# New SBUF start addresses for the operand tiles of the matrix products in a two-layer hybrid decoder

## The chip, the cores and the metric

The kernel runs on one core of a Trainium2 chip. The metric is device time in microseconds (us) of one execution: the median of three runs of the kernel before is 1026.87 us (1026.75 to 1027.55).

## The reference

A trunk of two layers on 256 tokens with 1024 channels, all in float32. Layer 0 mixes tokens with two recurrences (RG-LRU and HGRN2), layer 1 with a Mamba-2 state-space mixer. Each layer then has cross-attention into 256 memory tokens and a squared-ReLU MLP. Nearly all arithmetic is products of a 256-row activation with weight matrices:

```python
for l in range(DEPTH):                                   # 2 layers
    h = rmsnorm(x, norm_mix_g[l])
    if l % 2 == 0:
        proj = h @ e_w_in[e]                             # 1024 x 6144
        ...                                              # rg_lru, hgrn2_mix
        mix = jnp.concatenate([ya, yb], axis=-1) @ e_w_out[e]     # 2048 x 1024
    else:
        z, xbc, dt_raw = jnp.split(h @ o_w_in[o], O_SPLITS, axis=-1)
        ...                                              # mamba2_mix
        mix = ym @ o_w_out[o]                            # 2048 x 1024
    x = x + mix
    x = x + mem_cross_attn(rmsnorm(x, ...), rmsnorm(mem, ...), xq_w[l], xk_w[l], xv_w[l], xo_w[l])
    hf = rmsnorm(x, norm_ffn_g[l])
    x = x + jnp.square(jax.nn.relu(hf @ ffn_w1[l])) @ ffn_w2[l]   # 1024 x 4096, 4096 x 1024
return rmsnorm(x, final_norm_g)
```

## The kernel before

**Operands in two parts.** Every float32 operand of a large product is split in two float32r numbers, high and low, so that a product is three matmuls: high x high, high x low, low x high. A weight half-chunk (128 partitions x 1024 numbers, 512 KiB) is loaded by SyncE's queue into a tile `raw` (`Stream.loading`, line 150). ScalarE copies it into `wh` (line 164) and VectorE subtracts to make `wl` (line 165). There are four `raw` buffers and five each of `wh` and `wl`; loads and splits run a fixed number of halves ahead of the products. Activations are split in the same way into `nh`, `nl` (normalized inputs of a block, four buffers each) and `yh`, `yl` (outputs of mixers, attention and MLP, eight buffers each). Each such buffer holds two tiles of 128 x 256, 2 KiB per partition.

**The products.** `gemm` (lines 451, 453, 454) keeps 128 columns of a weight part in the array and streams 256 tokens of an activation part past them: for each k-tile of 128 channels and each 128 columns, one matmul with `wh` and the high activation part, one with `wh` and the low part, one with `wl` and the high part. Each of them loads its weights anew. `gemm_nat` (lines 470 to 472) turns this around: 128 tokens of an activation part are stationary and 512 columns of a weight part stream. A weight half-chunk has 24 matmuls of the first kind or 12 of the second. The order of the instructions is made by the framework's scheduler from the program's order, with short chains of steps put between the products; inside a product it is fixed (`seq`).

**Where tiles lie.** Pools take SBUF in the order in which they are opened: `cst` (constants, the residual stream `xres`), `wp` (`raw`, `wh`, `wl`), `ap` (all other working tiles), then `l0` or `l1` (one layer's own). Within a pool each buffer follows the one before. So the constants decide where the weight tiles begin. In the built program, in bytes along a partition:

| tiles | first buffer at | each buffer | start modulo 512 | modulo 64 |
|---|---|---|---|---|
| `raw`, `wh`, `wl` (pool `wp`) | 30,272 | 4,096 | 64 | 0 |
| `yh`, `yl` (pool `ap`) | 108,128 | 2,048 | 96 | 32 |
| `nh`, `nl` (pool `ap`) | 177,024 | 2,048 | 384 | 0 |

A matmul reads 512 bytes (128 stationary numbers) and 1,024 or 2,048 bytes (256 or 512 streamed numbers) per partition, and these pieces start at the tile's start plus a multiple of 512.

Of the kernel before, what the change touches and what calls it, by code (L numbers as in the profile page):

```python
# [16 lines left out]
P = 128  # L17
D = 1024
T = 256
# [5 lines left out]

# halves of weight chunks: buffers as loaded and as split, how far ahead they are split, and loaded before that
RAW_BUFS, PART_BUFS, SPLIT_AHEAD, LOAD_AHEAD = 4, 5, 3, 4
# chunks of layer 1's memory keys and values before the groups of the state-space mixer, and with each of them
KV_FIRST, *KV_EACH = 2, 2, 2, 2, 0, 0, 0, 0, 0
# how far short chains are taken ahead of the program's order  # L30
AHEAD = 200

# ---------------------------------------------------------------- the order of the weight chunks
# A chunk is 128 x (kt * cols) with kt * cols = 2048 (or less): kt k-tiles of a block of columns.

# [72 lines left out]

# ---------------------------------------------------------------- columns of the table of small parameters
_FIRST = [("memkv", 16), ("mix", 16)]  # L110
# [15 lines left out]
class Stream:  # L126
    """The halves of the weight chunks in their order: load, and split in two float32r parts."""

# [14 lines left out]
    def loading(self):  # L143
        """the next half, a piece at a time"""
        h = self.loaded
        self.loaded += 1
        hk, n = self._shape(h)
        self.raw[h] = raw = self.pool.tile([P, 1024], F32, tag="raw", bufs=RAW_BUFS, name=f"raw{h // 2}_{h % 2}")
        for a, b in self._pieces(h, hk * n):
            self.nc.sync.dma_start(raw[:, a:b], self.wst[h // 2, h % 2, :, a:b])  # L150
            yield
# [27 lines left out]
    def ahead(self, h):  # L179
        """what goes on while half h is multiplied"""  # L180
        with self.tc.high_priority(offset=0):
            self.split(h + 1 + SPLIT_AHEAD)
            self.load(h + 1 + SPLIT_AHEAD + LOAD_AHEAD)
# [7 lines left out]
class Pipe:  # L191
    """Chains of small steps that are issued a step at a time between the large products."""

# [19 lines left out]
def trunk(ctx: ExitStack, tc: tile.TileContext, wst, small, levels, gatew, xT, memT, fing, out):  # L213
# [3 lines left out]
    cst = ctx.enter_context(tc.tile_pool(name="cst", bufs=1))  # L217
    wp = ctx.enter_context(tc.tile_pool(name="wp", bufs=1))
    ap = ctx.enter_context(tc.tile_pool(name="ap", bufs=1))
    ps = ctx.enter_context(tc.tile_pool(name="ps", bufs=1, space=PSUM))  # L220
# [10 lines left out]
    def sc(i, name, shape=(P, 2, 256)):  # L231
        """scratch, two tiles of 2 KiB for each number"""
        return gt(name, f"s{i}", 2, shape)

    def nhl():
        return gt("nh", "nh", 4, dt=F32R), gt("nl", "nl", 4, dt=F32R)

    def yhl():
        return gt("yh", "yh", 8, dt=F32R), gt("yl", "yl", 8, dt=F32R)

# [25 lines left out]

    onesr = cst.tile([P, 128], F32R, name="onesr")
    def xpair(p):
        return xres[:, 2 * p:2 * p + 2, :]

    # ---------------------------------------------------------------- small helpers
    def seq():
        return tc.manual_schedule(engines={PE.engine})

    def order(after, before, why):
        """two instructions of one engine, in this order"""
        tc.add_manual_dep(after.ins, before.ins.name, NOSYNC, reason=why)
# [19 lines left out]
    def diag(r):  # L297
        """diagonal matrices of the two columns of r, in two parts"""
        dh, dl = (gt(t, t, 2, (P, 2, 128), F32R) for t in ("dgh", "dgl"))
        with tc.high_priority(offset=AHEAD):  # L300
            for j in range(2):
                V.tensor_scalar(dh[:, j, :], ident, r[:, j:j + 1], None, ALU.mult)
            for j in range(2):
                V.scalar_tensor_tensor(dl[:, j, :], ident, r[:, j:j + 1], dh[:, j, :].bitcast(F32),
                                       ALU.mult, ALU.subtract)
        return dh, dl
# [10 lines left out]
    def token_sums(sq, o, fold):  # L317
        """o[:, half] = the sum over channels of sq [channels, 2, tokens]"""
        n = 1 if fold else 2
# [27 lines left out]
    def gained(hl, src, gain, i0):  # L347
        """src * gain (a column for each of the two tiles) in two parts"""
        h, lo = hl
# [6 lines left out]
    class Norm:  # L356
        """x * gain in two float32r parts, and 1 / rms of every token."""

# [18 lines left out]
        def add(s, xp, p, parts=True):  # L377
            """a chain of steps for one pair of tiles"""
            parts = parts and s.gain is not None
# [33 lines left out]
        def apply(s, xp, p):  # L413
            """the norm applied before the projection"""
            h = sc(3, "hx")
# [9 lines left out]

    # ---------------------------------------------------------------- products with the weights
    def chunk(label, piece, ticks=1, rows=1):
# [14 lines left out]
    def gemm(label, os, H, L, k0=0, first=True, last=True, ticks=1):  # L442
        """os[pair][:, j, :] += W[:, 128 columns of each]^T x over the k-tiles of a chunk"""
        kt = PLAN[st.pos][3]
# [19 lines left out]
    def gemm_nat(label, os, H, L, k0=0, first=True, last=True, ticks=1):  # L464
        """os[half] += x[tokens of the half]^T W over the k-tiles of a chunk, tokens on partitions"""
        kt = PLAN[st.pos][3]
# [8 lines left out]

    # ---------------------------------------------------------------- memory keys and values
    kT, vN = [[], []], [[], []]

    class Memory:
# [13 lines left out]
        def step(s, ticks=1):  # L493
            """the next chunk of the keys, then of the values"""
            i, l, n = s.done, s.l, s.n
# [76 lines left out]

    # ---------------------------------------------------------------- parameters of layer 0's mixers
    def pt():
# [33 lines left out]
    def conv(o, wn, bn, tiles, stride, cv):  # L608
        """width-4 causal depthwise convolution of two tiles"""
        r = sc(cv, "cv")  # L610
# [7 lines left out]

    # ---------------------------------------------------------------- RG-LRU
    def rglru(p, xc, ga):  # L620
# [33 lines left out]

    # ---------------------------------------------------------------- HGRN2
    sts = []
# [8 lines left out]
    def hgrn(p, F, K, q, Q, vg):  # L665
        """scores by halves of blocks of 2, 4, ... 256 tokens; every decay is a product of forget gates"""
        Qf, Kf, Tm = flat(Q), flat(K), flat(F)
# [114 lines left out]

    # ---------------------------------------------------------------- parts that both layers have
    def residual(o, p, nrm):
# [6 lines left out]
    def out_deep(label, H, L, nrm, ticks=1):  # L791
        """x += W^T y, 16 k-tiles in two sweeps over four accumulators"""
        os = [pg() for _ in range(4)]
        for kh in range(2):
            for p in range(4):
                gemm(f"{label}_{kh}{p}", [os[p]], H, L, 8 * kh, kh == 0, kh == 1, ticks)
                if kh == 1:
                    residual(os[p], p, nrm)

    def products(o, pairs):  # L800
        """o = the sum of the products of (stationary, moving), each in two float32r parts"""
        last = len(pairs) - 1
# [5 lines left out]
    def parted(i, name, src):  # L808
        """two float32r parts of src"""
        h, lo = (gt(f"{name}{c}", f"s{i + c}", 2, dt=F32R) for c in range(2))  # L810
# [102 lines left out]

    # ---------------------------------------------------------------- layer 0
    pipe.drain()
# [12 lines left out]

    # ---------------------------------------------------------------- layer 1
    pipe.spawn(m1.prepare())  # L930
# [30 lines left out]
    def steps(o):  # L961
        """dt, and the sums of dt * A within each half of the tokens"""
        with tc.high_priority(offset=AHEAD):
# [30 lines left out]
    def decays(g):  # L994
        """exp(sum over s+1..t of dt A) of four heads, [s, (s0 t0 | s0 t1 | s1 t1)]"""
        E = l1.tile([P, 4, 3, 128], F32, tag="E", bufs=2, name=nm("E"))
# [27 lines left out]
    def ssd(g, E, xs, bc, z):  # L1024
        gap = 3 if g < 7 else 2
        for _ in range(gap):
            yield
        # masked C B^T, and x * dt with tokens on partitions
        cb = pm((P, 512))
# [83 lines left out]

    # ---------------------------------------------------------------- the last sum and norm, with tokens on partitions
    xn = [[sc(4 + 2 * hf + c, "xn", (P, 512)) for c in range(2)] for hf in range(2)]
# [3 lines left out]
    def turn():  # L1119
        """x with tokens on partitions, and the last gain for all of them"""  # L1120
        for c in range(2):
# [61 lines left out]

# ---------------------------------------------------------------- layout on the host

# [65 lines left out]
```

## Time and profile before

| what | value |
|---|---|
| median of three runs | 1026.87 us |
| the profiled execution: first to last instruction (span) | 1024.7 us |
| TensorE matmul busy (PE) | 1012.2 us, 99% of the span, 8485 matmuls |
| TensorE weight load busy (PEld) | 958.2 us, 94% |
| VectorE (DVE) / ScalarE (ACT) busy | 773.8 us / 610.4 us |
| DMA | 180.54 MB, mean 176 GB/s |
| granted TensorE clock | full (9 in each of the 40 slices) |

How to read it: a matmul's shown length (0.28 us) includes the time that it spends in the array's pipeline, beside the next one; what a stream of matmuls costs is the distance from start to start. A row of the timeline is start, length, engine, line, operation and its tiles, in the form out<-moving,stationary for `gemm` (the page writes the operand that streams first).

### The profile page before, as it was taken

What the parts mean: (1) busy time and instruction counts of PE and PEld (TensorE: products, weight loads), DVE (VectorE), ACT (ScalarE), POOL (GpSimd) and SP (SyncE); (2) the same over time, 40 slices, a digit from 0 to 9 for tenths busy, and PEclk for the clock granted to TensorE, in tenths of its full rate; (3) what the DMA queues carried; (4) which work ended last, traced back from release to release, by engine and by line L of the source; (5) the groups of instructions that cost most, each with busy time, mean ns of one, the idle gap of its engine ahead of it and who ended that gap; (6) DMA issues with size and microseconds to landing.
All of it is one profiled execution on the core that took longest, in us unless ns stands there. A gap on an engine that the chain in (4) does not pass through costs nothing.

```text
span 1024.7 us, 20857 instructions
## 1 busy us (share of the span) xinstructions
PE 1012.2 (99%) x8485; PEld 958.2 (94%) x8485; DVE 773.8 (76%) x1471; ACT 610.4 (60%) x886; POOL 1.2 (0%) x6
## 2 busy tenths in 40 slices
PE   8999999999999999999999999999999999999997
PEld 7898988989999999999999999999999999889985
DVE  7968788786887864565699888999989786546653
ACT  6667757674566653464546876778456656535542
POOL 0000000000000000000000000000000000000000
PEclk9999999999999999999999999999999999999999
DMA  8764443444544555555546665444545355555551
GB/s 292 273 218 157 140 150 135 175 146 146 183 145 166 185 185 185 186 187 187 173 150 219 217 189 202 169 162 144 206 135 195 129 166 181 185 185 185 187 184 41
DMA packets 52560, 180.54 MB, mean 176 GB/s; under 512 B 5968, under 2 KB 6128, under 8 KB 52336
## 3 DMA queue, kind: packets, MB, share of 16 engines
q1 hardware_dynamic: 52176, 178.69, 51.8%
q8 instruction: 66, 1.08, 0.4%
q10 hardware_dynamic: 288, 0.52, 0.1%
q14 instruction: 30, 0.25, 0.1%
HBM read 178.11 MB, written 1.08 MB: 175 GB/s over the span
## 4 chain that ended last, share of the span: by engine, by line
PE 90%; DVE 4%; ACT 4%; issue 1%; DMA 1%; SPq 0%; ACTq 0%
PE pg L451 23%; PE pg L453 22%; PE pg L454 22%; PE pg L472 4%; PE pg L470 4%; PE pg L471 4%; DVE wl L165 1%; ACT wh L164 1%; PE pm L325 1%; PE pm L1052 1%; PE pm L804 1%; PE pm L805 1%; PE pm L806 1%; DMA raw<-in_wst_dram 1%; PE pm L675 1%
## 5 line engine op out<-in xcount | busy, mean ns | idle before, releaser
L164 ACT CAST wh<-raw 128x1024 fp32r<-128x1024 f32 (+1 forms) x325 | 336.2, 1038 | 322.9 <-PE pg L453 219.9
L165 DVE TENSOR_TENSOR wl<-raw,wh 128x1024 fp32r<-128x1024 f32 (+1 forms) x325 | 391.4, 1209 | 164.6 <-ACT wh L164 163.9
L451 PE MATMUL pg<-nh,wh 128*128 128x256 f32 x1280 | 362.4, 283 | 0.0
L453 PE MATMUL pg<-nl,wh 128*128 128x256 f32 x1280 | 357.8, 280 | 0.0
L454 PE MATMUL pg<-nh,wl 128*128 128x256 f32 x1280 | 357.1, 279 | 0.0
L451 PEld LDWEIGHTS pg<-nh,wh 128*128 128x128 f32 x1280 | 240.5, 188 | 1.7 <-issue 0.7
L453 PEld LDWEIGHTS pg<-nl,wh 128*128 128x128 f32 x1280 | 240.1, 188 | 0.3
L454 PEld LDWEIGHTS pg<-nh,wl 128*128 128x128 f32 x1280 | 240.1, 188 | 0.0
L451 PE MATMUL pg<-yh,wh 128*128 128x256 f32 x768 | 215.4, 281 | 1.3 <-ACT yh L367 0.7
L453 PE MATMUL pg<-yl,wh 128*128 128x256 f32 x768 | 215.0, 280 | 0.1
L454 PE MATMUL pg<-yh,wl 128*128 128x256 f32 x768 | 214.7, 280 | 0.3 <-DVE wl L165 0.2
L451 PEld LDWEIGHTS pg<-yh,wh 128*128 128x128 f32 x768 | 144.3, 188 | 2.3 <-ACT wh L164 1.3
L454 PEld LDWEIGHTS pg<-yh,wl 128*128 128x128 f32 x768 | 144.2, 188 | 1.0 <-DVE wl L165 0.7
L453 PEld LDWEIGHTS pg<-yl,wh 128*128 128x128 f32 x768 | 144.3, 188 | 0.7 <-DVE yl L374 0.3
L470 PE MATMUL pg<-wh,yh 128*128 128x512 f32 x176 | 69.9, 397 | 0.0
L472 PE MATMUL pg<-wl,yh 128*128 128x512 f32 x176 | 69.6, 396 | 0.0
L471 PE MATMUL pg<-wh,yl 128*128 128x512 f32 x176 | 69.6, 395 | 0.0
L615 DVE SCALAR_TENSOR_TENSOR cv<-pg,smB,cv 128x255 f32<-128x255 f32 (+2 forms) x120 | 49.2, 473 | 0.5 <-ACT cv L612 0.5
L470 PEld LDWEIGHTS pg<-wh,yh 128*128 128x128 f32 x176 | 33.1, 188 | 7.9 <-issue 0.3
L472 PEld LDWEIGHTS pg<-wl,yh 128*128 128x128 f32 x176 | 33.1, 188 | 7.9
L471 PEld LDWEIGHTS pg<-wh,yl 128*128 128x128 f32 x176 | 33.1, 188 | 7.6
L896 DVE SCALAR_TENSOR_TENSOR t<-pg,rb 128x512 f32<-128x512 f32 x32 | 21.9, 690 | 16.5 <-PE pg L454 16.5
(262 smaller groups left out, 1097.5 us busy)
## 6 DMA issues: line engine op xcount, KB each, us to landing
raw<-in_wst_dram SPq DMA_DIRECT2D x317, 512.0 KB, 3.3
ac<-acd SPq DMA_DIRECT2D x16, 256.0 KB, 4.8
mem<-in_memT_dram SPq DMA_DIRECT2D x8, 256.0 KB, 4.4
raw<-in_wst_dram SPq DMA_DIRECT2D x8, 256.0 KB, 4.5
xres<-in_xT_dram SPq DMA_DIRECT2D x4, 256.0 KB, 6.4
gw<-in_gatew_dram SPq DMA_DIRECT2D x1, 1024.0 KB, 7.6
smB<-in_small_dram SPq DMA_DIRECT2D x1, 545.0 KB, 6.9
gn<-in_fing_dram SPq DMA_DIRECT2D x2, 256.0 KB, 3.8
```

The source lines that it names most:

```text
L164: self.last = nc.scalar.copy(hi[:, a:b], raw[:, a:b])
L165: nc.vector.tensor_tensor(lo[:, a:b], raw[:, a:b], hi[:, a:b].bitcast(F32), ALU.subtract)
L325: PE.matmul(o[:, hf:hf + 1], sq[:, c, 128 * hf:128 * hf + 128], ones[:, :1], start=(c == 0), stop=(c == n - 1))
L451: PE.matmul(o[:, j, :], wh[:, cs], xh, start=(first and k == 0 and j == 0), stop=False, skip_group_check=True)
L453: PE.matmul(o[:, j, :], wh[:, cs], xl, start=False, stop=False, skip_group_check=True)
L454: PE.matmul(o[:, j, :], wl[:, cs], xh, start=False, stop=(last and k == kt - 1), skip_group_check=True)
L470: PE.matmul(os[j], h, wh, start=(first and k == 0), stop=False)
L471: PE.matmul(os[j], lo, wh, start=False, stop=False)
L472: PE.matmul(os[j], h, wl, start=False, stop=(last and k == kt - 1))
L615: V.scalar_tensor_tensor(r[:, j, i:], o[:, j, :256 - i], col(wn, (3 - i) * stride + c), r[:, j, i:], ALU.mult, ALU.add)
L675: PE.matmul(tgt[32 * j:32 * j + 32, b // 4, :], Kf[:, 32 * b:32 * b + 32], qq[:, 32 * b:32 * b + 32], start=True, stop=True, tile_position ...
L896: V.scalar_tensor_tensor(t, o, 0.0, b2(n.rb), ALU.max, ALU.mult)
```

## The change

A filler tile of 624 numbers (2,496 bytes) is put at the place of `cst` where it moves the later small constants and the pool `wp` behind them. `nh`, `nl`, `yh` and `yl` are no longer tiles of `ap` but of a new pool `mp`, opened between `wp` and `ap`. Shapes, types and numbers of buffers are the same. (The file after also has fewer comments, which shifts no instruction.)

```diff
+PAD = 624
...
     wp = ctx.enter_context(tc.tile_pool(name="wp", bufs=1))
+    mp = ctx.enter_context(tc.tile_pool(name="mp", bufs=1))
     ap = ctx.enter_context(tc.tile_pool(name="ap", bufs=1))
...
+    def part(name, bufs):
+
+        return mp.tile([P, 2, 256], F32R, tag=name, bufs=bufs, name=nm(name))
+
     def nhl():
-        return gt("nh", "nh", 4, dt=F32R), gt("nl", "nl", 4, dt=F32R)
+        return part("nh", 4), part("nl", 4)
 
     def yhl():
-        return gt("yh", "yh", 8, dt=F32R), gt("yl", "yl", 8, dt=F32R)
+        return part("yh", 8), part("yl", 8)
...
     onesr = cst.tile([P, 128], F32R, name="onesr")
+
+    cst.tile([P, PAD], F32, name="pad")
```

In the built program the order of the instructions on every engine, with their waits, is the same row for row before and after; only addresses differ. `raw` now begins at 32,768, `wh` at 49,152 and `wl` at 69,632 (all multiples of 4,096); `yh` at 90,112, `yl` at 106,496, `nh` at 122,880 and `nl` at 131,072 (all multiples of 2,048). So all seven start at 0 modulo 512 and modulo 64, and a 256-number stream no longer runs over a multiple of 1,024. The tiles left in `ap` begin at 139,264 and are still at multiples of 32 bytes; the two-part operands of the attention products, among them, start at 32 or 320 modulo 512 where they started at 96 or 384.

## Rows read from the trace of the kernel before

**Rows 1.** Page, parts 1 and 4: busy time; the chain that ended last.

```profile
PE 1012.2 (99%) x8485; PEld 958.2 (94%) x8485; DVE 773.8 (76%) x1471; ACT 610.4 (60%) x886; POOL 1.2 (0%) x6
...
PE 90%; DVE 4%; ACT 4%; issue 1%; DMA 1%; SPq 0%; ACTq 0%
```

**Rows 2.** Groups by line and shape: count, busy us, mean ns, idle before.

```profile
L451 PE MATMUL pg<-nh,wh 128*128 128x256 f32 x1280 | 362.4, 283 | 0.0
L451 PE MATMUL pg<-yh,wh 128*128 128x256 f32 x768 | 215.4, 281 | 1.3 <-ACT yh L367 0.7 <-ACT wh L164 0.6
L470 PE MATMUL pg<-wh,yh 128*128 128x512 f32 x176 | 69.9, 397 | 0.0
L470 PE MATMUL pg<-wh,nh 128*128 128x512 f32 x64 | 26.0, 406 | 0.0
```

**Rows 3.** Timeline of PE, layer 0's MLP: start us, length us, engine, line.

```profile
378.72 0.28 PE L451 MATMUL pg<-yh,wh 128*128 128x256 f32 x1
...
423.51 0.28 PE L451 MATMUL pg<-nh,wh 128*128 128x256 f32 x1
...
468.74 0.28 PE L451 MATMUL pg<-yh,wh 128*128 128x256 f32 x1
```

**Rows 4.** Timeline of PE, layer 1's projections of the second group.

```profile
561.25 0.28 PE L454 MATMUL pg<-nh,wl 128*128 128x256 f32 x1
...
571.68 0.28 PE L453 MATMUL pg<-nl,wh 128*128 128x256 f32 x1
```

**Rows 5.** Busy time by stretch: us, then each engine's busy us (count).

```profile
378.72:423.52 44.80, 44.80 (x387) 44.80 (x386) 23.02 (x21) 17.91 (x18) 0.00 (x0) 1.00 0.55 189
423.52:468.74 45.22, 45.22 (x386) 45.22 (x385) 29.72 (x31) 24.86 (x30) 0.00 (x0) 1.00 0.57 187
561.26:571.68 10.42, 10.42 (x94) 10.42 (x93) 6.79 (x16) 10.39 (x17) 0.00 (x0) 1.00 0.71 229
```

**Rows 6.** Timeline of PE, end of layer 1's output projection.

```profile
771.46 0.28 PE L451 MATMUL pg<-yh,wh 128*128 128x256 f32 x1
...
774.28 0.28 PE L451 MATMUL pg<-nh,wh 128*128 128x256 f32 x1
```

**Rows 7.** Timeline of PE, layer 1's last product.

```profile
982.62 0.40 PE L470 MATMUL pg<-wh,yh 128*128 128x512 f32 x1
982.85 0.40 PE L471 MATMUL pg<-wh,yl 128*128 128x512 f32 x1
983.08 0.40 PE L472 MATMUL pg<-wl,yh 128*128 128x512 f32 x1
983.32 0.40 PE L470 MATMUL pg<-wh,yh 128*128 128x512 f32 x1
```

**Rows 8.** Timeline of PE and PEld, layer 0's MLP.

```profile
425.28 0.28 PE L451 MATMUL pg<-nh,wh 128*128 128x256 f32 x1
425.29 0.19 PEld L453 LDWEIGHTS pg<-nl,wh 128*128 128x128 f32 x1
425.40 0.28 PE L453 MATMUL pg<-nl,wh 128*128 128x256 f32 x1
```

**Rows 9.** Timeline of PE, layer 1's attention products (operands in `ap`).

```profile
798.78 0.28 PE L806 MATMUL pm<-pl,kv 128*128 128x256 f32 x1
...
799.38 0.28 PE L805 MATMUL pm<-ph,kv 128*128 128x256 f32 x1
```

**Rows 10.** Waits: who waited for whom, us in total, times, longest.

```profile
ACT wh L164 <- PE pg L453: 219.9, 155, 3.4
DVE wl L165 <- ACT wh L164: 163.9, 171, 3.6
...
ACT wh L164 <- DMA raw<-in_wst_dram: 21.2, 14, 4.9
```

## The prediction

> **What bounds the kernel now.** I read the shares and the chain first, then the groups by shape, then the timeline of TensorE alone. The first shows one bound: matmuls fill 99% of the span and the chain runs over PE for 90% of it, with DVE and ACT at 4% each [rows 1]. The groups give the mass: of the kind with 256 streamed columns there are 3 x (1280 + 768) = 6144, of the kind with 512 columns 3 x (176 + 64) = 720, and their idle time is about nothing [rows 2]. The mean length in these rows is no price, since lengths overlap. The price is the distance from start to start, so the view to read is the timeline at the two ends of a stretch without pauses. Layer 0's MLP has such stretches, 8 weight chunks of 48 matmuls each. From 378.72 to 423.51 the streamed tiles are `yh` and `yl`: 44.79 us / 384 = 116.6 ns each. From 423.51 to 468.74 they are `nh` and `nl`: 45.23 us / 384 = 117.8 ns [rows 3]. [...]
>
> [...] Only this pace can move the time much: 1 ns on the 256-column kind is 6.1 us.
>
> Does the pace know addresses? Three things in the trace bear on it. First, the two long stretches differ by 1% with the same instructions and the same clock [rows 3, 5]; what differs is the streamed tile, at 96 modulo 512 for `yh` and 384 for `nh`. Second, the same tiles do not always have the same pace: `nh`, `nl` run 92 matmuls from 561.25 to 571.68 in 10.43 us, 113.4 ns each [rows 4] (the count of 94 for that stretch holds two that began earlier) [rows 5]. And `yh`, `yl` have a stretch of 24 in 2.82 us, 117.5 ns, in layer 1 [rows 6]. So there are a few steady paces (113.4, 116.6, 117.8), a stretch falls into one and keeps it, and the streamed tile's address seems to say which are open to it. Third, the weight load of the next matmul starts 0.01 us behind the start of the one that streams [rows 8]: two reads of SBUF, 512 and 1,024 bytes, run side by side all the time, and their places relative to each other are what this change moves.
>
> **The change part by part.** No instruction is added, removed or moved, so there is no wait to add and no stall to remove; there are only changed addresses.
>
> *Weight parts to 0 modulo 512 (from 64), `nh`, `nl` from 384 and `yh`, `yl` from 96 to 0.* The nearest rows are the paces themselves. `nh`, `nl` and the weights are already at multiples of 64, and their usual pace is 117.8. `yh`, `yl` are 32 off; they become like `nh`. I take it that the multiple of 64 is what tells the two classes apart, since the classes agree in all smaller powers of two. Then everything falls into the paces of `nh`: 117.8 mostly, 113.4 now and then. The price: `yh`, `yl` fill six blocks of 384, each 45.23 - 44.79 = 0.44 us slower, +2.6 us at most; some of their stretches are at the slow pace already [rows 6], and a stretch may fall into 113.4. On the other side the fast stretches of `nh` could be lost: I know of 92 [rows 4], worth 92 x 4.4 ns = 0.4 us, and allow twice that. So between 0 and +3.4 us; the middle, +1.7, is my value.
>
> The ends for this edit, if larger multiples matter: at the fast end all 256-column matmuls at 113.4, which is 2304 x 3.2 + 3840 x 4.4 ns = 7.4 + 16.9 = -24 us, and with the 512-column kind better in the same ratio (3.5% of 168) -30 us. At the slow end 120 ns, the pace of the attention products (five matmuls in 0.60 us) [rows 9], whose operands lie at other offsets: 2304 x 3.4 + 3840 x 2.2 ns = 7.8 + 8.4 = +16 us.
>
> [...]
>
> *`raw` to a multiple of 4,096 (from 64 modulo 512).* ScalarE waits for a `raw` transfer 21.2 us in all, 14 times [rows 10], while it waits 219.9 us for TensorE to release buffers. Transfers are ahead nearly everywhere, the DMA share is 0.55 in the MLP [rows 5], and the first chunks wait for bytes from memory, not for their place. I take 0; the bounds are -1 and +1 us, 5% of the 21.2.
>
> *Tiles that stay in `ap`.* DVE and ACT are busy 23 and 18 us of 44.8 in the first stretch [rows 5] and wait for PE: a slower access is hidden there. The attention products, 192 matmuls, move among offsets; at 3 ns each way that is 0.6 us. I take 0.
>
> Sum: +1.7 us on the profiled execution's 1024.7. The runs lie 2.1 us above that span (launch and end outside it), which the change leaves alone. So 1026.87 + 1.7 = 1028.6 us.
>
> **Rivals.**
>
> *Fast pace.* Aligned pieces let both reads run in step, and the 113.4 becomes the rule [rows 4]. For it: that pace exists for 92 matmuls in a row, with tiles at multiples of 128 streaming, and never in the two long `yh` and `nh` blocks. Against it: the same addresses give 117.8 for 384 in a row, so something besides addresses chooses. Whole, the time is 1027 - 24 to 30, about 1000; VectorE and ScalarE have room for it, about half busy [rows 5], so nothing takes it back. In part (one of the two classes, or `nh` at 116.6: 3840 x 1.2 ns = 4.6 us) it is 1005 to 1023; I take 1015.
>
> *Collision, on the slower side.* All pieces start at 0 modulo 512, and stream and weight load start within 0.01 us of each other [rows 8], so both reads begin at the same offset at the same moment, in every matmul. If one has to give way there, the pace goes to 120 or beyond [rows 9]: 1027 + 16 = 1043; half of it 1035. It decides from a mean of 0.33 ns more per matmul, 2.05 us in all. [...] Against it: the attention's mixed offsets give 120 too, so equal offsets are not needed for that pace.
>
> [...]
>
> *Nothing happens.* The pace is set by when a stretch starts, not where its tiles lie, and the mix of paces comes out the same: 1026.9. For it: both classes leave their usual pace in places [rows 4, 6].
>
> **How the numbers follow.** Everything like `nh` (forecast): 0.37. Fast pace whole 0.19, in part 0.19. Collision 0.16. Nothing 0.09. About 0.2% (2.05 us) is what a measurement of this kernel can tell from no change. The forecast's own range is 1026.5 to 1030.5, and it is worth 0.22 of same, 0.13 of slower and 0.02 of faster. With the fast cases faster is 0.40; with nothing, same is 0.31; with the collision, slower is 0.29. For the range I take in half of the whole fast pace and all but the worst of the collision: 1001 to 1037 us.
>
> **What would show it.** The matmul counts, the order and the wait groups stay. Right: the block of `yh`, `yl` from about 379 us takes 45.2 us for 384 instead of 44.8, the `nh` block still 45.2, and three 512-column matmuls 0.70 us. Fast pace: the blocks take 43.5 us. Collision: 46 us or more in both. Wrong beyond the rivals would be a time that moves while the blocks stay: then it would sit in the first 60 us (transfers) or in the attention.

## The result and the profile after

The changed kernel takes 1036.93 us (median of four runs, 1036.78 to 1037.10) against 1026.81 us: ratio 1.0096, 95% interval 1.0083 to 1.0108. It is about 1% slower. The forecast of 1028.6 us was the likeliest case and did not come; the range of 1001 to 1037 us held the time at its very end, and of the rivals it is the collision whose sign came, 46 us in both blocks.

The page of the kernel after, parts 1 and 4, answers to [rows 1]:

```profile
PE 1023.6 (99%) x8485; PEld 975.1 (94%) x8485; DVE 774.6 (75%) x1471; ACT 610.6 (59%) x886; POOL 1.2 (0%) x6
...
PE 93%; DVE 3%; ACT 3%; issue 1%; DMA 0%; SPq 0%; ACTq 0%
```

The counts are the same, DVE and ACT are busy for the same time as before, and PE is busy for 11.4 us more. The span grew by 10.6 us (1035.3 against 1024.7). So look at the blocks of [rows 3], in the timeline of PE (start us, length us, engine, line; L460 is what L451 was):

```profile
382.28 0.28 PE L460 MATMUL pg<-yh,wh 128*128 128x256 f32 x1
...
428.36 0.28 PE L460 MATMUL pg<-nh,wh 128*128 128x256 f32 x1
...
474.44 0.28 PE L460 MATMUL pg<-yh,wh 128*128 128x256 f32 x1
```

Both blocks of 384 matmuls now take 46.08 us, 120.0 ns each, where it was 44.79 and 45.23. The difference between the two classes is gone, and so is every faster pace in them. The clock is not the cause; busy time by stretch (us, then each engine's busy us and count, last the granted clock, DMA share and GB/s) shows it at 1.00, as in [rows 5], with DVE, ACT and DMA as they were:

```profile
382.28:428.36 46.08, 46.08 (x387) 46.08 (x385) 23.02 (x21) 17.91 (x18) 0.00 (x0) 1.00 0.56 183
428.36:474.44 46.08, 46.08 (x387) 46.08 (x385) 29.73 (x31) 24.85 (x30) 0.00 (x0) 1.00 0.55 183
```

The matmuls with 512 streamed columns went the other way. Three of them took 0.70 us [rows 7]; now, in the same product:

```profile
992.14 0.39 PE L479 MATMUL pg<-wh,yh 128*128 128x512 f32 x1
992.36 0.39 PE L480 MATMUL pg<-wh,yl 128*128 128x512 f32 x1
992.59 0.39 PE L481 MATMUL pg<-wl,yh 128*128 128x512 f32 x1
992.82 0.39 PE L479 MATMUL pg<-wh,yh 128*128 128x512 f32 x1
```

0.68 us, 226.7 ns each. The balance, if every matmul ran at the pace of its kind here: 6 blocks of `yh`, `yl` at 46.08 - 44.79 = +1.29 us, 10 blocks of `nh`, `nl` at 46.08 - 45.23 = +0.85 us, together +16.2; 720 x (233.3 - 226.7 ns) = -4.8; sum +11.4 us against +10.6 in the span. Added up from start to start over the whole trace, pauses included, the 256-column kind takes 14.5 us more, the 512-column kind 3.7 us less and all other matmuls 0.2 us less: these are the 10.6 us.

The waits (who waited for whom: us in total, times, longest) are those of [rows 10] with PE released later:

```profile
ACT wh L166 <- PE pg L462: 231.3, 158, 3.5
DVE wl L167 <- ACT wh L166: 169.2, 174, 4.5
...
ACT wh L166 <- DMA raw<-in_wst_dram: 16.6, 13, 4.4
```

### The profile page after: what moved, and what is told of

It is laid out like the page before. It is cut to its first block, busy times and chain, and to the rows that moved or that the text cites. A ratio compares the mean times of both kernels' runs of the same rounds, so it can differ in the third digit from the quotient of the medians.

```text
span 1035.3 us, 20857 instructions
## 1 busy us (share of the span) xinstructions
PE 1023.6 (99%) x8485; PEld 975.1 (94%) x8485; DVE 774.6 (75%) x1471; ACT 610.6 (59%) x886; POOL 1.2 (0%) x6
## 4 chain that ended last, share of the span: by engine, by line
PE 93%; DVE 3%; ACT 3%; issue 1%; DMA 0%; SPq 0%; ACTq 0%
PE pg L460 24%; PE pg L462 23%; PE pg L463 23%; PE pg L481 4%; PE pg L480 4%; PE pg L479 4%; PE pm L334 1%; PE pm L1061 1%; ACT wh L166 1%; PE pm L684 1%; PE pm L813 1%; DVE wl L167 1%; PE pm L814 1%; PE pm L815 1%; PE pm L321 0%
## 5 line engine op out<-in xcount | busy, mean ns | idle before, releaser
L166 ACT CAST wh<-raw 128x1024 fp32r<-128x1024 f32 (+1 forms) x325 | 335.8, 1037 | 328.0 <-PE pg L462 231.3
L460 PE MATMUL pg<-nh,wh 128*128 128x256 f32 x1280 | 366.7, 286 | 0.0
L462 PE MATMUL pg<-nl,wh 128*128 128x256 f32 x1280 | 362.2, 283 | 0.0
L463 PE MATMUL pg<-nh,wl 128*128 128x256 f32 x1280 | 361.9, 283 | 0.0
L460 PEld LDWEIGHTS pg<-nh,wh 128*128 128x128 f32 x1280 | 245.1, 191 | 1.6 <-issue 0.7
L462 PEld LDWEIGHTS pg<-nl,wh 128*128 128x128 f32 x1280 | 245.3, 192 | 0.3
L463 PEld LDWEIGHTS pg<-nh,wl 128*128 128x128 f32 x1280 | 245.2, 192 | 0.0
L460 PE MATMUL pg<-yh,wh 128*128 128x256 f32 x768 | 219.1, 286 | 0.6 <-ACT wh L166 0.6
L460 PEld LDWEIGHTS pg<-yh,wh 128*128 128x128 f32 x768 | 148.1, 193 | 1.5 <-ACT wh L166 1.4
L462 PEld LDWEIGHTS pg<-yl,wh 128*128 128x128 f32 x768 | 148.2, 193 | 0.3 <-issue 0.2
L463 PEld LDWEIGHTS pg<-yh,wl 128*128 128x128 f32 x768 | 147.9, 193 | 0.5 <-DVE wl L167 0.2
```

The source lines that it names most:

```text
L166: self.last = nc.scalar.copy(hi[:, a:b], raw[:, a:b])
L460: PE.matmul(o[:, j, :], wh[:, cs], xh, start=(first and k == 0 and j == 0), stop=False, skip_group_check=True)
L462: PE.matmul(o[:, j, :], wh[:, cs], xl, start=False, stop=False, skip_group_check=True)
L463: PE.matmul(o[:, j, :], wl[:, cs], xh, start=False, stop=(last and k == kt - 1), skip_group_check=True)
```

## The experiments

Two theories stood against each other. **A**: the pace depends on the *distance* between the streamed and the stationary piece, their start addresses taken modulo some power of two. **B**: the pace depends on the multiples at which pieces begin, each by itself. The kernel after has both distance 0 and aligned pieces, so it does not tell them apart. Its two halves, each alone, do. In all kernels only addresses differ; distance is the start of the activation part less that of the weight part, modulo 512.

**One half: the pool without the filler (distance 0, nothing aligned).**

```diff
-PAD = 624
+PAD = 0
...
-    cst.tile([P, PAD], F32, name="pad")
```

> The pool for the activation parts without the filler tile: weight parts stay at 64 modulo 512, and all activation parts come to 64 modulo 512 too. Distance between the streamed and the stationary piece: 0, as in the changed kernel, but nothing begins at a multiple of 128 or more. Theory A (only the distance between the two pieces counts; at distance 0 the two reads collide): like the changed kernel, 1037 us, 256-column matmuls at 120.0 ns, 512-column ones at 226.7 ns. Theory B (the multiples at which pieces begin count by themselves): like the kernel before, 1024 to 1030 us, 116.6 to 117.8 ns and 233 ns.

Measured: 1037.16 us, ratio to before 1.0098 (1.0081 to 1.0115). The blocks take 46.08 us each:

```profile
381.85 0.28 PE L459 MATMUL pg<-yh,wh 128*128 128x256 f32 x1
...
427.93 0.28 PE L459 MATMUL pg<-nh,wh 128*128 128x256 f32 x1
...
474.01 0.28 PE L459 MATMUL pg<-yh,wh 128*128 128x256 f32 x1
```

The whole loss is there with every piece at 64 modulo 512, as theory A expected.

**The other half: the filler without the pool (weights aligned, old distances).**

```diff
-        return mp.tile([P, 2, 256], F32R, tag=name, bufs=bufs, name=nm(name))
+        return gt(name, name, bufs, dt=F32R)
```

> The filler tile without the pool: weight parts at multiples of 4096, activation parts still in the old pool, where the filler moves them to 32 (yh, yl) and 320 (nh, nl) modulo 512: the distances of the kernel before, 32 and 320, at other places. Theory A (distance): like the kernel before, 1025 to 1029 us, 116.6 ns with yh/yl and 117.8 ns with nh/nl, 233 ns with 512 columns. Theory B (aligned weights are what costs): 1032 to 1037 us, since all weight loads now begin at multiples of 512; at least the 512-column ones, which stream the weights, go to 227 ns.

Measured: 1026.33 us, ratio 0.9998 (0.9988 to 1.0007). The first two blocks are those of the kernel before, 44.81 and 45.22 us. The third, which streams `yh` again, is not:

```profile
378.07 0.28 PE L460 MATMUL pg<-yh,wh 128*128 128x256 f32 x1
...
422.88 0.28 PE L460 MATMUL pg<-nh,wh 128*128 128x256 f32 x1
...
468.10 0.28 PE L460 MATMUL pg<-yh,wh 128*128 128x256 f32 x1
...
514.06 0.28 PE L463 MATMUL pg<-yh,wl 128*128 128x256 f32 x1
```

The 383 steps from 468.10 to 514.06 take 120.0 ns each. The kernel before makes the same steps, from 468.74 [rows 3], at 116.7 ns:

```profile
513.42 0.28 PE L454 MATMUL pg<-yh,wl 128*128 128x256 f32 x1
```

A stretch of 238 steps with `nh`, `nl` in layer 1's MLP goes the other way. Here it takes 113.4 ns a step,

```profile
855.80 0.28 PE L462 MATMUL pg<-nl,wh 128*128 128x256 f32 x1
...
882.78 0.28 PE L463 MATMUL pg<-nh,wl 128*128 128x256 f32 x1
```

and in the kernel before 117.8 ns:

```profile
854.65 0.28 PE L453 MATMUL pg<-nl,wh 128*128 128x256 f32 x1
...
882.69 0.28 PE L454 MATMUL pg<-nh,wl 128*128 128x256 f32 x1
```

So one distance can have more than one pace, and these two stretches (+1.3 and -1.1 us) cancel in the total. The first two blocks keep the pace that they had (116.7 and 117.8 ns), and the 512-column matmuls, which theory B sends to 227 ns, stay at 233.3.

All weight tiles were moved to multiples of 4,096 and the time did not move. Theory B falls with these two runs: the four combinations of weights (64 or 0) and distance (old or 0) give 1026.8, 1037.2, 1026.3 and 1036.9 us, so the time goes with the distance and not with the weights' place.

**Which distances.** A tile of some bytes ahead of the activation parts sets the distance; this is the edit for 64, the others differ in the number (24, 32, 40, 48, 56):

```diff
     cst.tile([P, PAD], F32, name="pad")
+    mp.tile([P, 16], F32, name="shift")
```

> The changed kernel with 64 bytes put ahead of the activation parts: weight parts at 0, activation parts at 64 modulo 512, distance 64. Theory A with a period of 512 (or 128): the collision at the common start is gone, 256-column pace 113 to 118 ns, time 1003 to 1029 us. Theory A with a period of 64: nothing changes, 120 ns and 1037 us. Theory B: the weights are still aligned, the streams are not; between 1027 and 1037 us, and the 512-column ones keep 227 ns.

Measured: 1027.81 us, ratio 1.0008 (0.9998 to 1.0017). Both blocks run at 117.8 ns, 45.23 and 45.22 us:

```profile
378.78 0.28 PE L461 MATMUL pg<-yh,wh 128*128 128x256 f32 x1
...
424.01 0.28 PE L461 MATMUL pg<-nh,wh 128*128 128x256 f32 x1
...
469.23 0.28 PE L461 MATMUL pg<-yh,wh 128*128 128x256 f32 x1
```

This is the case of the forecast, both blocks at the pace of `nh`, `nl`, at the time of the forecast less 0.8 us. A period of 64 is out.

For 256 bytes the filler is left out, so the weights stay at 64 modulo 512:

```diff
-PAD = 624
+PAD = 0
...
-    cst.tile([P, PAD], F32, name="pad")
+    mp.tile([P, 64], F32, name="shift")
```

> Pool without filler, 256 bytes ahead of the activation parts: weight parts at 64, activation parts at 320 modulo 512, distance 256. Theory A with a period of 512: no collision at the start, 113 to 118 ns, 1003 to 1029 us. Theory A with a period of 256 or less: 120 ns and 1037 us. Theory B: nothing is aligned, like the kernel before, 1024 to 1030 us.

Measured: 1037.52 us, ratio 1.0104 (1.0089 to 1.0119): both blocks 46.08 us, 512-column matmuls at 226.9 ns. Distance 256 is distance 0; a period of 512 is out, and 128 or 256 is left.

The distances that follow are set with the filler in place. Distance 128:

> The changed kernel with 128 bytes ahead of the activation parts: distance 128 between streamed and stationary pieces. Distances 0 and 256 gave 120.0 ns, 64 gave 117.8 with stretches of 113.3. Period 128: collision again, 120.0 ns and 226.7 ns, 1037 us. Period 256: the farthest that two pieces can be from each other, 113 to 118 ns, 233 ns for 512 columns, 1004 to 1029 us.

Measured: 1036.93 us, ratio 1.0095 (1.0078 to 1.0112). The time is that of distance 0, but this is chance: the 512-column matmuls are at 232.4 ns, not 226.7, and layer 1's MLP block of 384 with `nh` takes 45.56 us (118.6 ns) where it takes 46.07 (120.0 ns) at distance 0. The time alone would have misled to a period of 128.

Distance 96:

> Distance 96. Period 128: it is 32 short of a collision; if only the size of the distance to the next collision counts, it is like 32, which yh/yl had before: 116.7 ns, about 1022 us with all tiles there. Period 256: a new place between 64 and 128, 113 to 118 ns, 1004 to 1029 us.

Measured: 1042.04 us, ratio 1.0147 (1.0132 to 1.0163), the slowest: 120.0 ns with 256 columns and 234 ns with 512:

```profile
383.30 0.28 PE L461 MATMUL pg<-yh,wh 128*128 128x256 f32 x1
...
429.38 0.28 PE L461 MATMUL pg<-nh,wh 128*128 128x256 f32 x1
...
475.46 0.28 PE L461 MATMUL pg<-yh,wh 128*128 128x256 f32 x1
```

Neither expectation had it. The distance to the next collision is not the rule.

Distance 160:

> Distance 160. Period 128: the same as 32, 116.7 ns with all 256-column matmuls, about 1022 us. Period 256: another place, 113 to 118 ns, 1004 to 1029 us, not necessarily the paces of 32.

Measured: 1029.97 us, ratio 1.0030 (1.0018 to 1.0041): blocks of 45.06 and 45.05 us, 117.3 ns. Not the pace of 32, which speaks against a period of 128.

Distance 192:

> Distance 192. Period 128: the same as 64, measured at 1027.8 us: 117.8 ns with some 113.3. Period 256: 64 short of a collision, so the weight read runs ahead of the streaming read instead of behind it; if the sign of the distance counts the paces differ from those of 64, else they are the same.

Measured: 1013.06 us, ratio 0.9866 (0.9851 to 0.9880): the blocks at 113.3 ns. The same blocks take 45.2 us at 64. Alone this would not rule out a period of 128: at 64 some stretches keep 113.3 ns too, and at 192 some keep 117.8.

Distance 224:

> Distance 224, that is 32 short of the next collision at 256. Distance 192 gave 1013.06 us, with 113.3 ns in more than half of the stretches and 117.8 in the rest. If the pace gets better on the whole way from 160 to 256: 113.3 ns nearly everywhere, 1002 to 1010 us. If 192 is a place of its own, as 64 and 96 were next to each other with 117.8 and 120.0: 116 to 120 ns, 1020 to 1040 us.

Measured: 1032.32 us, ratio 1.0049 (1.0034 to 1.0064): blocks of 45.44 us, 118.3 ns:

```profile
380.58 0.28 PE L461 MATMUL pg<-yh,wh 128*128 128x256 f32 x1
...
426.02 0.28 PE L461 MATMUL pg<-nh,wh 128*128 128x256 f32 x1
...
471.46 0.28 PE L461 MATMUL pg<-yh,wh 128*128 128x256 f32 x1
```

192 is a place of its own. And 96 and 224 are 128 bytes apart and keep different paces in both blocks (120.0 and 118.3 ns), so the period is not 128. The sign counts too: 96 and 160 lie 96 bytes on either side of a multiple of 256, and their blocks run at 120.0 and 117.3 ns.

**The test of the period, and the version that beats both.** Without the filler, with 448 bytes ahead:

```diff
-PAD = 624
+PAD = 0
...
-    cst.tile([P, PAD], F32, name="pad")
+    mp.tile([P, 112], F32, name="shift")
```

> No filler, weight parts at 64 modulo 512; 448 bytes ahead of the activation parts, which puts them at 0 modulo 512: distance 448, which is 192 modulo 256. Theory A with a period of 256 (only the distance counts): like the distance 192, 1010 to 1016 us, with 113.3 and 117.8 ns. A period of 512, or alignment as such: anything else, most simply the 1027.8 us of distance 64, which is as far from a multiple of 512, or the 1037 us of activations at 0.

Measured: 1012.05 us (1010.88 to 1013.11), ratio 0.9848 (0.9831 to 0.9864). The blocks take 43.52 us each, 113.3 ns:

```profile
374.66 0.28 PE L460 MATMUL pg<-yh,wh 128*128 128x256 f32 x1
...
418.18 0.28 PE L460 MATMUL pg<-nh,wh 128*128 128x256 f32 x1
...
461.70 0.28 PE L460 MATMUL pg<-yh,wh 128*128 128x256 f32 x1
```

Here the activation parts are at 0 modulo 512, as in the changed kernel, and the weights are where they were before. 448 is 192 modulo 256: distances 192 and 448 agree as 0 and 256 do. This kernel is 1.5% faster than before, without one instruction changed. Its gain is in the matmuls: PE is busy for 997.9 us instead of 1012.2, and ScalarE, with the same busy time, waits 208.5 us for the release by PE instead of 219.9 [rows 10].

```profile
ACT wh L166 <- PE pg L462: 208.5, 155, 4.2
```

Four of the runs also settle that neither place counts by itself. With the weights at 64 modulo 512, the activation parts at 64 and at 0 give 1037.2 and 1012.1 us; with the weights at 0, they give 1027.8 and 1036.9. Moving the activation parts gains in the one case and costs in the other.

All distances together (block times from the timeline as above, of the first `yh` and the first `nh` block; in the filler-only run the second `yh` block takes 46.08; the last column is the mean start-to-start time over 143 steps of the last product, 33.35 us before):

| kernel | distance modulo 256 | time, us | `yh` block, us | `nh` block, us | 512 columns, ns |
|---|---|---|---|---|---|
| after, pool only, shift 256 | 0 | 1036.9, 1037.2, 1037.5 | 46.08 | 46.08 | 226.9 |
| before, filler only | 32 (`yh`), 64 (`nh`) | 1026.8, 1026.3 | 44.80 | 45.22 | 233.3 |
| shift 64 | 64 | 1027.8 | 45.23 | 45.22 | 233.4 |
| shift 96 | 96 | 1042.0 | 46.08 | 46.08 | 234.3 |
| shift 128 | 128 | 1036.9 | 46.08 | 46.08 | 232.4 |
| shift 160 | 160 | 1030.0 | 45.06 | 45.05 | 233.3 |
| shift 192, shift 448 | 192 | 1013.1, 1012.1 | 43.52 | 43.52 | 228.9 |
| shift 224 | 224 | 1032.3 | 45.44 | 45.44 | 233.3 |

**Each pair of reads, or the stretch as a whole?** In the best kernel the low parts get a pool of their own, at distance 0:

```diff
+    ml = ctx.enter_context(tc.tile_pool(name="ml", bufs=1))
...
-        return mp.tile([P, 2, 256], F32R, tag=name, bufs=bufs, name=nm(name))
+        return (mp if name in ("nh", "yh") else ml).tile([P, 2, 256], F32R, tag=name, bufs=bufs, name=nm(name))
...
+    ml.tile([P, 16], F32, name="shift2")
```

> Weight parts at 64 modulo 512; high activation parts (nh, yh) at 0, distance 448 (192 modulo 256), the best so far at 1012.05 us; low activation parts (nl, yl) in a pool of their own at 64, distance 0. One matmul in three streams a low part. Each pair of reads by itself: the matmuls that stream a low part take 120.0 ns, the others keep 113 to 118 ns, mean 117 ns, about 1022 us. The stretch as a whole, because a delay in one matmul shifts the next: the other two lose the 113.3 ns as well, 118 to 120 ns, 1029 to 1037 us.

Measured: 1031.23 us, ratio 1.0045 (1.0030 to 1.0059). The blocks take 45.79 and 45.80 us, 119.2 ns. Six steps at the start of the first block take 0.71 us, 118 ns each, and no third of them stands out:

```profile
380.23 0.28 PE L462 MATMUL pg<-yh,wh 128*128 128x256 f32 x1
380.35 0.28 PE L464 MATMUL pg<-yl,wh 128*128 128x256 f32 x1
380.47 0.28 PE L465 MATMUL pg<-yh,wl 128*128 128x256 f32 x1
380.58 0.28 PE L462 MATMUL pg<-yh,wh 128*128 128x256 f32 x1
380.70 0.28 PE L464 MATMUL pg<-yl,wh 128*128 128x256 f32 x1
380.82 0.28 PE L465 MATMUL pg<-yh,wl 128*128 128x256 f32 x1
380.94 0.29 PE L462 MATMUL pg<-yh,wh 128*128 128x256 f32 x1
```

Over all neighbouring matmuls with no pause between them the three steps are 119.1 ns (high part with `wh`), 119.3 (low part) and 117.1 (high part with `wl`). With a third of the matmuls at distance 0 all three steps are slower than in the best kernel, whose mean is 115.1 ns.

The opposite has the high parts at distance 0, with the low ones' pool set 448 bytes on:

```diff
-    mp.tile([P, 112], F32, name="shift")
-    ml.tile([P, 16], F32, name="shift2")
+    ml.tile([P, 112], F32, name="shift2")
```

> The opposite: high activation parts at distance 0 of the weight parts, low ones at 448. Two matmuls in three stream a high part. Each pair by itself: 120.0 ns for two, 113 to 118 ns for one, mean 118.5 ns, about 1029 us. The stretch as a whole: like distance 0 everywhere, 120.0 ns for all three, 1035 to 1037 us.

Measured: 1028.82 us, ratio 1.0019 (1.0010 to 1.0029): the figure expected of independent pairs, but not for their reason. The blocks run at 117.8 ns (45.22 and 45.23 us), and the steps are 118.3, 118.0 and 117.3 ns, not 120.0 twice and 113 to 118 once. With two thirds at distance 0 the kernel is faster than with one third there. So at distance 0 the 120.0 belongs to a stretch in which every pair has that distance, and not to a single matmul. Neither theory held for both mixtures: the first came as the stretch theory expected (1029 to 1037 us), the second did not (1035 to 1037).

## Why the prediction was right or wrong

- **What bounds the kernel: right.** Only the start-to-start time of the large matmuls moved. The attention and the `raw` transfers, costed at 0 to 1 us, did not show: transfers still land in 3.3 us (median), and weights at multiples of 4,096 left the time alone in the filler-only run (1026.33 us, ratio 0.9998).
- **That the pace knows addresses, and that two reads side by side are what the change moves: right.** The pool-only run and the ones that set the distance show that the distance of the two pieces moves the pace: same instructions, the same granted clock (0.998 to 0.999 in every run), and blocks from 113.3 to 120.0 ns by addresses alone. The filler-only run shows that the distance does not settle it alone (116.7 and 120.0 ns at one distance). What makes the pace follow the distance, no run here shows.
- **The failed step** is "I take it that the multiple of 64 is what tells the two classes apart". It was chosen as one of several powers of two, and the trace of before could not choose: its two classes are only distances 32 and 320. What tells them apart in the runs is the distance modulo 256, and 320 is 64 there. With all parts at multiples of 64 the blocks run at 113.3, 117.8 or 120.0 ns, by the distance. The step's own sum was good for the case that it describes: with distance 64 both blocks do run like `nh`, `nl`, at 1027.8 us where 1028.6 was said. The changed kernel has distance 0 instead.
- **The collision rival** had the place, the pace and the price per matmul: 120.0 ns and +16.2 us on the 256-column kind. Its sum had no term for the 512-column kind, which went the other way (-4.8 us by the same blocks). That is most of why the time is 1037 and not 1043. Its mechanism is not shown. "Both reads begin at the same offset at the same moment" fits distance 0, but distances 96 and 128 give 120.0 too, where they do not begin together.
- **Against the collision** it was said that the attention's mixed offsets give 120 as well. That row could not carry it: by the addresses in the built program two in three of these products are at distance 32 and one in three at distance 0 modulo 256, so equal offsets are among them.
- **The fast pace** was a rival with the wrong condition. The 113.4 of [rows 4] can become the rule, and is worth 14.8 us (1026.87 to 1012.05), but by a distance of 192, not by alignment. The 168 us in the sum of its fast end are 720 x 233 ns [rows 7]. No run shows the 3.5% taken there for the 512-column kind: with the blocks at 113.3 ns it runs at 228.9 ns, 1.9% less than before, and its best is 226.7 (2.8%), at distance 0.
- **The range** held the time by 0.07 us, and that is luck: the forecast was +1.7 us and +10.1 came. At the collision's own price for the 256-column kind the time would have been 1043, outside the range; the 512-column kind, which no sum of the slow side held, brought it back in. The chance of slower, 0.29, looks too low afterwards: of eight distances tried in steps of 32 (32 and 64 mixed, as before), four cost more than 0.4%, and one gains.
- **Two readings were off at no cost.** The executions lie 1.7 to 1.8 us above their own spans, not 2.1. And the 720 leave out the 48 matmuls of 512 columns that end layer 1's last product.

Open: why a distance has the pace that it has; distances between the multiples of 32 bytes that were tried; and what chooses between two paces at one distance (below).

## What to carry to other kernels

Where matmuls run back to back, compare the start-to-start times of stretches that stream different tiles: a difference at one clock (here 116.6 and 117.8 ns) is a hint that addresses matter. Scan then the distance between streamed and stationary tiles in steps of 32 bytes up to 256 (the period found here), with a dummy tile in a pool, before aligning anything (alignment made all distances 0 here, a bad place for 256 columns: 120.0 ns against 113.3 at 192), and judge the scan by the paces of long stretches and not by the total, where two kinds can cancel and give a false match.

## What the hardware showed that was not expected

- The pace of these products depends on the two operands' distance, and every pair of distances tried that agree modulo 256 bytes agrees in time or pace: 0 and 256 agree (1036.9 to 1037.5 us), 192 and 448 agree (1013.1 and 1012.1), 64 gives `yh` the pace that 320 gave `nh`, while 64 and 192 do not agree, nor do 0 and 128 in all their paces.
- The kinds want different distances: 0 is among the worst for 256 columns (120.0 ns) and the best for 512 (226.7 ns). In the 512-column kind the weights stream, so there the distance from the stationary to the streamed piece has the other sign.
- One distance can have two steady paces, as the filler-only run showed at 32 (116.7 and 120.0 ns). In the best kernel, 264 matmuls of layer 0's output projection keep 117.8 ns (31.09 us), 104 us before those that keep 113.3 with the same tiles' offsets, at full clock:

```profile
239.05:270.14 31.09, 31.09 (x266) 31.09 (x265) 20.57 (x25) 15.91 (x21) 0.00 (x0) 1.00 0.54 187
374.66:418.18 43.52, 43.52 (x387) 43.52 (x385) 23.02 (x21) 18.03 (x18) 0.00 (x0) 1.00 0.56 194
418.18:461.70 43.52, 43.52 (x387) 43.52 (x385) 29.69 (x31) 24.92 (x30) 0.00 (x0) 1.00 0.56 194
```

In the best kernel each of these two paces holds for its whole stretch, 31.09 us at 117.8 ns and 87.04 us at 113.3. A pause before a stretch is not the whole account of its pace: the two `yh` blocks of the filler-only run, at 116.7 and 120.0 ns, both begin without one, 0.11 us after the start of the matmul before. If all stretches of this kernel kept 113.3 ns instead of 115.1, its mean over the pairs without a pause between them, it would save another 6144 x 1.8 = 11 us, by an estimate from these two paces; how to enter the faster one was not tried.
